# A step of fill after every step of the sample tokens' recurrence, and its eight-column products split in four

## The chip, the cores and the metric

The kernel runs on one core of one Trainium2 chip. The metric is the device time of one execution in microseconds (us), from the first to the last of the core's work. The engines carry the names of the profile: PE is TensorE's matmuls, PEld its weight loads, DVE is VectorE, ACT ScalarE, POOL GpSimd, SP SyncE. Weights and activations go through the DMA queues of SP and ACT.

## The reference, cut to what matters

One layer of a hybrid decoder works on 1024 prompt tokens and on 8 sample sequences of 4 tokens each. An FFN is followed by one wide projection `w_in`, whose columns feed four mixers (gated linear attention, a gMLP, an RWKV-7 recurrence, dilated attention); `w_out` joins them and a second FFN ends the layer. The change touches the recurrence alone, and of it the sample tokens:

```python
def step(S, xs):
    r_t, w_t, k_t, v_t, a_t, b_t = xs
    sa = jnp.einsum('bhvk,bhk->bhv', S, a_t)
    S = S * w_t[:, :, None, :] + sa[..., None] * b_t[:, :, None, :] + v_t[..., None] * k_t[:, :, None, :]
    return S, jnp.einsum('bhvk,bhk->bhv', S, r_t)
...
s_final, y = lax.scan(step, s0.astype(f32), (tm(r), tm(decay), tm(k), tm(v), tm(-kk), tm(kk * a)))
```

For the sample tokens `s0` is a given state per sequence and head (8 sequences, 4 heads, 64 x 64), and the scan has four steps.

## The kernel before, in words

**Three thirds and a fill.** The big products (`w_in`, `w_out`, the FFNs) run with the weight as the stationary operand in 128 x 128 pieces and 352 tokens as the moving one. Each product is made three times, as high part by high part, high by low and low by high (`mm3`, L131 to L145; the trace shows them as L139, L142 and L143). In `w_in` the 37 column blocks of 128 are tiles of the generator `line` (L2821): for each block and each third of the tokens, eight K pieces of three matmuls, with a yield after every second piece. So one step of this fill is 6 matmuls of 128 x 352, a third is 4 steps, and a tile is 12. After a third, `leave` (L2774) copies the result out of PSUM and stores it; during a tile the weight of the next is split by `part` (ACT L111, POOL L112) and that of the one after it is loaded. The blocks come in the order of `W_ORDER` (L2718): 8 for the recurrence, 4 for the gMLP, 6 of dilated group 2, 7 for the linear attention, then 12 of dilated groups 1 and 0, q, k and v for each pair of heads. Tile 33 waits until the recurrence and the gMLP are through (L2849, `L.mixed == 2`). Behind the last tile the fill goes on with half of `w_out`, the products `pz` at L2897 (128 x 256), and ends there; what follows has to wait for the mixers.

**The loom.** The order in which the program issues its instructions is made at build time by `Loom` (L1399). It keeps a model of when each engine is free and when each tile is written, and has a list of generators, the streams, each with a priority and a time at which it is next ready. `run` (L1574) goes round: if `cool()` says that the modelled flow of columns through TensorE in the last 3.4 us is small, it takes a step of the fill (`weft`, L1530); else the best of the streams that are ready makes a step; if none is ready, the fill makes one. On DVE and POOL the order so made is pinned in this part of the kernel (`keep(KR)`, L3088); on PE and ACT it is the order of issue, in which the build may still move single instructions.

**The recurrence.** `rwkv` (L1127) runs the prompt in four pieces of 256 tokens and the sample tokens as a fifth. Three streams are live: the two pairs of heads (`pairs(0)`, `pairs(1)`, L1340) and `feeder` (L1329), which prepares and finishes pieces. `pairs` hands each step of `unit` or `sample` on as a condition (L1354 to L1357); what these yield is used only as a further condition, and a number among it counts as none.

**The sample tokens.** `sample` (L1763) is a chain of short steps per pair: load the state (L1779), turn it (L1783), the token-by-token products (L1790), three transposes (L1795 to L1797), a 32 x 32 inverse (L1808 to L1820), its uses (L1824 to L1841), then the products of the state with the 8 columns of each sequence (L1849): for each of the two heads, 8 matmuls of 64 x 64 by 64 x 8, whose results two copies on ACT take out (L1851, L1852). The new state is made by L1856 to L1873, and L1878 to L1882 turn it and store it. There are 16 yields in it. A step's matmuls are small, its result goes through ACT or DVE before the next step can start, and the two pairs take turns, with fill between them where the loom puts it.

**What follows.** After the recurrence come the linear attention and the dilated attention (`gla`, `dil`) with the rest of the fill, at their end the sample tokens' attention over the caches (L2347, four matmuls for each of 36 loaded cache pieces), then the other half of `w_out` (L204) and the second FFN.

Of the kernel before, what the change touches and what calls it, by code (L numbers as in the profile page):

```python
# [1398 lines left out]
class Loom:  # L1399
# [4 lines left out]
    def __init__(self, tc, fill):  # L1404
        self.tc, self.ins = tc, tc.nc.cur_bb.bb.instructions
        self.i, self.last = len(self.ins), {}
        self.free, self.wrote, self.used, self.slots, self.red = {}, {}, {}, {}, {}
        self.fill, self.done, self.over = fill, {}, False
        self.live, self.hold, self.due = [], None, 0.0
        self.fresh, self.marks = [], []  # L1410
        self.ticks, self.flow, self.cells = {}, [], [0.0] * 16
        self.pe = tc.nc.tensor.engine
        self.kept = ()

    def keep(self, engines):

        self.kept = [getattr(self.tc.nc, e).engine for e in engines]
# [156 lines left out]
    def run(self, until, others=True):  # L1574

        while not until():
            now = self.free.get(self.pe, 0.0)
            if others and self.cool() and self.weft():
                continue
            ok = [s for s in self.live if others and self.open(s, now)]  # L1580
            go = [s for s in ok if s[2] <= now + SLACK]
            if go:
                self.step(min(go, key=lambda s: s[0] - (now - s[2]) / AGE))
            elif not self.weft():
                self.free[self.pe] = min(t for t in [self.due] + [s[2] for s in ok] + list(self.done.values()) if t > now)
                self.cells = [max(t, self.free[self.pe]) for t in self.cells]
# [176 lines left out]
def sample(L, rp, C, p, AR, BK, vt, eL, y, ps):  # L1763

    nc, I, O, ident = L.nc, L.I, L.O, L.ident
    D2 = dict(bufs=2)
    A, R = AR[:, 0], AR[:, 1]
    BKf = BK.rearrange("p a t -> p (a t)")
    b4 = lambda x: x.rearrange("p (b i) -> p b i", i=4)
    tri = rp.tile([32, 3, 2, 32], F32, name="tri", tag="GN0", **D2)  # L1770
    Nn, N2, IN = tri[:, 0], tri[:, 1], tri[:, 2]
    rws = rp.tile([128, 96], F32, name="rws", tag="GN1", **D2)
    RW = rws[:, 0:64].rearrange("p (b a i) -> p b a i", b=8, a=2)
    SA = rws[:, 64:96]
    S0 = rp.tile([128, 8, 64], F32, name="S0", tag="AX", **D2)
    sv = [rp.tile([64, 4, 128], F32, name="sv", tag=t) for t in ("SA2", "rE")]
    for half in range(2):
        for h in range(2):
            L.dma(sv[half][:, :, 64 * h:64 * h + 64], I["state_rwkv"][0, 4 * half:4 * half + 4, 2 * p + h].rearrange("b v k -> v b k"))  # L1779
    yield  # L1780
    q = ps("pa")
    for b in range(8):
        nc.tensor.transpose(q[:, b * 64:(b + 1) * 64], sv[b // 4][:, b % 4, :], ident[:64, :64])  # L1783
    nc.scalar.copy(S0.rearrange("p b v -> p (b v)"), q)
    work = rp.tile([128, 2, 512], F32, name="work", tag="work", **D2)
    G = work[:64, 0, 0:128].rearrange("p (h a t) -> p h a t", h=2, a=2)
    for h in range(2):
        hr = slice(64 * h, 64 * h + 64)
        q = ps("pa")
        nc.tensor.matmul(q[:64, 0:64].rearrange("p (a t) -> p a t", a=2), BKf[hr], AR[hr], start=True, stop=True)  # L1790
        nc.vector.tensor_mul(G[:, h], q[:64, 0:64].rearrange("p (a t) -> p a t", a=2), C["mS"])

    yield
    q = ps("pa")
    nc.tensor.transpose(q[:64, 0:128], BKf, ident)  # L1795
    nc.tensor.transpose(q[:32, 128:256], A, ident)
    nc.tensor.transpose(q[:64, 256:384], vt[:, 32:96], ident)  # L1797
    NB = work[:64, 0, 128:256]
    nc.scalar.copy(NB, q[:64, 0:128])
    AX = rp.tile([32, 2, 128], F32, name="AXs", tag="BK", bufs=2)  # L1800
    nc.scalar.copy(AX[:, :, 0:64], q[:32, 128:256].rearrange("p (h k) -> p h k", h=2))
    UV = rp.tile([64, 2, 64], F32, name="UVs", tag="UV", **D2)
    nc.scalar.copy(UV[32:64], q[32:64, 256:384].rearrange("p (h k) -> p h k", h=2))

    yield
    q = ps("pa")
    for h in range(2):
        nc.tensor.transpose(q[:32, h * 32:(h + 1) * 32], G[0:32, h, 0, :], ident[:32, :32])  # L1808
    nc.scalar.copy(Nn, q[:32, 0:64].rearrange("p (h t) -> p h t", h=2))
    yield  # L1810
    q = ps("pa")
    for h in range(2):
        nc.tensor.matmul(q[:32, h * 32:(h + 1) * 32], G[0:32, h, 0, :], Nn[:, h, :], start=True, stop=True)
    nc.scalar.copy(N2, q[:32, 0:64].rearrange("p (h t) -> p h t", h=2))
    nc.vector.tensor_add(IN, G[0:32, :, 0, :], ident[:32, :32].unsqueeze(1).to_broadcast([32, 2, 32]))
    yield
    q = ps("pa")
    for h in range(2):
        nc.tensor.matmul(q[:32, h * 32:(h + 1) * 32], N2[:, h, :], IN[:, h, :], start=True, stop=True)
    nc.vector.tensor_add(IN, IN, q[:32, 0:64].rearrange("p (h t) -> p h t", h=2))  # L1820
    yield
    q = ps("pa")
    for h in range(2):
        nc.tensor.matmul(q[:32, h * 64:(h + 1) * 64], G[32:64, h, 0, :], UV[32:64, h, :], start=True, stop=True)  # L1824
    nc.scalar.copy(AX[:, :, 64:128], q[:32, 0:128].rearrange("p (h k) -> p h k", h=2))
    yield
    q = ps("pa")
    for h in range(2):
        nc.tensor.matmul(q[:32, h * 128:(h + 1) * 128], IN[:, h, :], AX[:, h, :], start=True, stop=True)
    q3 = q[:32, 0:256].rearrange("p (h x) -> p h x", h=2)  # L1830
    W = work[:32, 0, 256:384].rearrange("p (h k) -> p h k", h=2)
    nc.scalar.copy(W, q3[:, :, 0:64])
    nc.scalar.copy(UV[0:32], q3[:, :, 64:128])
    yield
    q = ps("pa")
    for h in range(2):
        nc.tensor.matmul(q[64 * h:64 * h + 64, 0:32], W[:, h, :], G[0:32, h, 1, :], start=True, stop=True)
    nc.vector.tensor_add(RW[:, :, 0, :], b4(q[:, 0:32]), b4(R))
    yield
    q = ps("pa")  # L1840
    nc.tensor.transpose(q[:, 0:32], W.rearrange("p h k -> p (h k)"), ident[:32, :32])  # L1841
    nc.scalar.copy(RW[:, :, 1, :], b4(q[:, 0:32]))
    yield

    for h in range(2):
        hr = slice(64 * h, 64 * h + 64)
        q = ps("pa")
        for b in range(8):
            nc.tensor.matmul(q[hr, b * 8:(b + 1) * 8], S0[hr, b, :], RW[hr, b], start=True, stop=True)  # L1849
        q4 = q[hr, 0:64].rearrange("p (b a i) -> p b a i", b=8, a=2)  # L1850
        nc.scalar.copy(b4(y[hr]), q4[:, :, 0, :])  # L1851
        nc.scalar.copy(b4(SA[hr]), q4[:, :, 1, :])  # L1852
    yield
    q = ps("pa")
    for h in range(2):
        nc.tensor.matmul(q[64 * h:64 * h + 64, 0:32], UV[:, h, :], G[:, h, 1, :], start=True, stop=True)  # L1856
    nc.vector.tensor_add(y, y, q[:, 0:32])
    yield
    q = ps("pa")
    nc.tensor.transpose(q[:32, 0:128], SA, ident)  # L1860
    nc.vector.tensor_add(UV[0:32], UV[0:32], q[:32, 0:128].rearrange("p (h v) -> p h v", h=2))
    exs = []
    for h in range(2):
        exs.append(rp.tile([64, 8, 64], F32, name="ex", tag=("SA2", "rE")[h]))
        nc.vector.tensor_mul(exs[h], UV[:, h, :].unsqueeze(1).to_broadcast([64, 8, 64]),
                             C["bm"].unsqueeze(2).to_broadcast([64, 8, 64]))
    yield
    q = ps("pa")
    for h in range(2):
        nc.tensor.matmul(q[64 * h:64 * h + 64, :], NB[:, 64 * h:64 * h + 64], exs[h].rearrange("p b v -> p (b v)"),  # L1870
                         start=True, stop=True)
    nc.vector.tensor_add(S0, S0, q.rearrange("p (b v) -> p b v", b=8))
    nc.vector.tensor_mul(S0, S0, eL.unsqueeze(2).to_broadcast([128, 8, 64]))  # L1873
    yield
    for half in range(2):
        q = ps("pa")
        for b in range(4):
            nc.tensor.transpose(q[:64, b * 128:(b + 1) * 128], S0[:, half * 4 + b, :], ident)  # L1878
        sv = rp.tile([64, 4, 128], F32, name="svo", tag=("spread", "SA2")[half])
        nc.scalar.copy(sv, q[:64].rearrange("p (b x) -> p b x", b=4))  # L1880
        for h in range(2):
            L.put(O["s_rwkv"][0, 4 * half:4 * half + 4, 2 * p + h].rearrange("b v k -> v b k"), sv[:, :, 64 * h:64 * h + 64])  # L1882
        yield


# [1294 lines left out]
```

## Time and profile before

| | |
|---|---|
| time before, median of 3 runs | 2499.52 us (2495.64 to 2504.91) |
| the profiled execution's own time | 2503.86 us |
| its span, first to last instruction | 2502.1 us |
| PE busy over the span | 2411.0 us, 96% |
| mean granted TensorE clock | 0.972 |
| sample tokens' first state load issued | 1264.31 us |
| first and last matmul of their steps (L1783, L1878) | 1270.49 and 1317.87 us |
| end of the fill (last `pz` matmul) | about 1630.7 us |
| other half of `w_out` begins (L204) | 1680.69 us |

Times inside the execution are counted from the start of its span. A row of a windows view gives, for a stretch, its length and then for each engine the busy time and in brackets how many instructions; behind them stand the granted TensorE clock (PEclk, 1.00 is full speed), the mean busy share of the DMA engines, and GB/s. A row of a timeline gives the start, the length, the engine and line, the operation, the tiles and the shape; `x4` means four instructions of one kind merged. A matmul's length holds its way through the array, so that the distance from one start to the next is what it costs in a row of its like.

### The profile page before, as it was taken

What the parts mean: (1) busy time and instruction counts of PE and PEld (TensorE: products, weight loads), DVE (VectorE), ACT (ScalarE), POOL (GpSimd) and SP (SyncE); (2) the same over time, 40 slices, a digit from 0 to 9 for tenths busy, and PEclk for the clock granted to TensorE, in tenths of its full rate; (3) what the DMA queues carried; (4) which work ended last, traced back from release to release, by engine and by line L of the source; (5) the groups of instructions that cost most, each with busy time, mean ns of one, the idle gap of its engine ahead of it and who ended that gap; (6) DMA issues with size and microseconds to landing.
All of it is one profiled execution on the core that took longest, in us unless ns stands there. A gap on an engine that the chain in (4) does not pass through costs nothing. (4 is left out here: it accounts for less than half of the span.)

```text
span 2502.1 us, 41009 instructions
## 1 busy us (share of the span) xinstructions
PE 2411.0 (96%) x15543; PEld 2207.7 (88%) x15543; DVE 1395.5 (56%) x3211; ACT 1013.6 (41%) x2175; POOL 1067.8 (43%) x902
## 2 busy tenths in 40 slices
PE   8999999999999999999999999968999999999997
PEld 8999999977789998898888899737989999997777
DVE  7645454367775056665632467437854444447767
ACT  5433333366554242323324344415533333336651
POOL 3655555567643233232111111114355555557664
PEclk9999999999999999999989889969999999999999
DMA  4322222323434333231226676444222222233334
GB/s 133 100 69 83 66 82 68 106 86 111 119 126 132 93 106 90 87 100 52 74 56 195 185 228 184 134 130 146 79 86 74 80 74 80 72 103 92 104 103 148
DMA packets 273612, 265.21 MB, mean 106 GB/s; under 512 B 36283, under 2 KB 247380, under 8 KB 273414
## 3 DMA queue, kind: packets, MB, share of 16 engines
q1 hardware_dynamic: 223810, 212.69, 28.9%
q10 hardware_dynamic: 49604, 49.90, 5.8%
q8 instruction: 122, 2.00, 0.3%
q14 instruction: 76, 0.62, 0.1%
HBM read 195.26 MB, written 67.16 MB: 105 GB/s over the span
## 5 line engine op out<-in xcount | busy, mean ns | idle before, releaser
L520 POOL TENSOR_TENSOR wlo<-wraw,whi 128x512 fp32r<-128x512 f32 x280 | 379.7, 1374 | 355.1 <-ACT whi L519 355.0
L549 PE MATMUL p<-xh,whi 128*128 128x352 f32 x1120 | 364.0, 325 | 5.4 <-DVE hid L475 3.6
L551 PE MATMUL p<-xh,wlo 128*128 128x352 f32 x1120 | 362.3, 323 | 0.0
L550 PE MATMUL p<-xl,whi 128*128 128x352 f32 x1120 | 361.2, 322 | 0.0
L519 ACT CAST whi<-wraw 128x512 fp32r<-128x512 f32 x280 | 166.5, 620 | 409.1 <-PE p L550 293.4
L112 POOL TENSOR_TENSOR wlo<-wraw,whi 128x1024 fp32r<-128x1024 f32 x61 | 146.0, 2396 | 391.8 <-ACT whi L111 343.6
L139 PE MATMUL pw<-xh,whi 128*128 128x352 f32 x888 | 308.1, 347 | 2.3 <-ACT stg L2782 1.5
L143 PE MATMUL pw<-xh,wlo 128*128 128x352 f32 x888 | 293.4, 330 | 0.0
L142 PE MATMUL pw<-xl,whi 128*128 128x352 f32 x888 | 293.1, 330 | 0.0
L549 PEld LDWEIGHTS p<-xh,whi 128*128 128x128 f32 x1120 | 211.4, 189 | 6.8 <-DVE hid L475 3.9
L550 PEld LDWEIGHTS p<-xl,whi 128*128 128x128 f32 x1120 | 211.5, 189 | 0.0
L551 PEld LDWEIGHTS p<-xh,wlo 128*128 128x128 f32 x1120 | 210.4, 188 | 0.0
L139 PEld LDWEIGHTS pw<-xh,whi 128*128 128x128 f32 x888 | 171.5, 193 | 13.3 <-issue 7.5
L142 PEld LDWEIGHTS pw<-xl,whi 128*128 128x128 f32 x888 | 172.1, 194 | 1.9 <-issue 1.7
L143 PEld LDWEIGHTS pw<-xh,wlo 128*128 128x128 f32 x888 | 171.2, 193 | 1.4 <-issue 1.2
L549 PE MATMUL p<-hid,whi 128*128 128x352 f32 x400 | 129.9, 325 | 1.8 <-ACT n L583 1.4
L551 PE MATMUL p<-hid,wlo 128*128 128x352 f32 x400 | 129.8, 324 | 1.4 <-POOL wlo L520 1.4
L550 PE MATMUL p<-hid,whi 128*128 128x352 f32 x400 | 129.2, 323 | 0.0
L111 ACT CAST whi<-wraw 128x1024 fp32r<-128x1024 f32 x61 | 63.9, 1048 | 118.7 <-PE pw L142 85.2
L723 PE MATMUL p<-xh,hid 128*128 128x512 f32 x320 | 109.8, 397 | 0.1
L204 PE MATMUL pt<-whi,ya 128*128 128x256 f32 x512 | 97.7, 290 | 1.0 <-POOL ya L793 1.0
L839 DVE TENSOR_TENSOR y<-y,p 128x512 f32<-128x512 f32 x112 | 76.6, 685 | 38.7 <-PE p L723 36.7
(641 smaller groups left out, 5861.9 us busy)
## 6 DMA issues: line engine op xcount, KB each, us to landing
wraw<-in_w_ff_gate_dram SPq DMA_DIRECT2D x44, 512.0 KB
wraw<-in_w_ff_up_dram SPq DMA_DIRECT2D x44, 512.0 KB
wraw<-in_w_in_dram SPq DMA_DIRECT2D x37, 512.0 KB
wraw<-in_w_ff_down_dram SPq DMA_DIRECT2D x36, 512.0 KB
hid_d<-tmp ACTq DMA_DIRECT2D x60, 176.0 KB
hid_d<-n ACTq DMA_DIRECT2D x60, 176.0 KB
cv<-in_cache_win_dram SPq DMA_DIRECT2D x36, 256.0 KB
whi<-hid_d SPq DMA_DIRECT2D x32, 256.0 KB
```

Of the source, the lines that this page charges most:

```text
L112: nc.gpsimd.tensor_tensor(lo, raw, hi.bitcast(F32), op=OP.subtract)
L139: ins = nc.tensor.matmul(out, a, xh[:, cs], start=(first and i == 0), stop=False)
L142: nc.tensor.matmul(out, a, xl[:, cs], start=False, stop=False)
L143: nc.tensor.matmul(out, b, xh[:, cs], start=False, stop=(last and i == n - 1))
L204: nc.tensor.matmul(out, xs[kx][a][:, cs], ws[js[0]][b][:, kw], start=u == a == b == 0, stop=u == len(kk) - 1 and a == 1, skip_group_check= ...
L519: nc.scalar.copy(t[0][:, i], v)
L520: nc.gpsimd.tensor_tensor(t[1][:, i], v, t[0][:, i].bitcast(F32), op=OP.subtract)
L549: nc.tensor.matmul(out, ah, xh, start=first and k == 0, stop=False, skip_group_check=True)
L550: nc.tensor.matmul(out, ah, xl, start=False, stop=False, skip_group_check=True)
L551: nc.tensor.matmul(out, al, xh, start=False, stop=k == KH - 1, skip_group_check=True)
L723: nc.tensor.matmul(out, a[i][:, u], b[j][:, u], start=first and u == i == j == 0, stop=u == n - 1 and i == 1, skip_group_check=True)
L839: (nc.vector.tensor_copy if h else nc.scalar.copy)(v, p) if copy else nc.vector.tensor_add(v, v, p)
```

## The change

The loom gets a flag, `thin`. When a step of `sample` has set it, the next turn of `run` takes a step of the fill first, whatever `cool()` says. Every yield of `sample` is preceded by `L.loom.thin = True`. In the loop over the 8 sequences a yield comes after every fourth matmul, so that for each head the 8 products are issued as 4 and 4, and the 16 of a pair in four groups. The copies of a head come after its second group. This makes 20 yields of 16. Instructions, tiles and operands are the same.

```diff
@@ Loom.__init__
         self.kept = ()
+        self.thin = False
@@ Loom.run
             now = self.free.get(self.pe, 0.0)
-            if others and self.cool() and self.weft():
+            thin, self.thin = self.thin, False
+            if others and (thin or self.cool()) and self.weft():
                 continue
@@ sample: ahead of each of its 16 yields
+    L.loom.thin = True
     yield
@@ sample, the products of the state
         for b in range(8):
             nc.tensor.matmul(q[hr, b * 8:(b + 1) * 8], S0[hr, b, :], RW[hr, b], start=True, stop=True)
+            if b % 4 == 3:
+                L.loom.thin = True
+                yield 0.0
```

More of the change, by code (lines that the diff above doesn't have):

```diff
@@ L1803, in sample @@
     nc.scalar.copy(UV[32:64], q[32:64, 256:384].rearrange("p (h k) -> p h k", h=2))
+    L.loom.thin = True
     yield
@@ L1809, in sample @@
     nc.scalar.copy(Nn, q[:32, 0:64].rearrange("p (h t) -> p h t", h=2))
+    L.loom.thin = True
     yield
@@ L1815, in sample @@
     nc.vector.tensor_add(IN, G[0:32, :, 0, :], ident[:32, :32].unsqueeze(1).to_broadcast([32, 2, 32]))
+    L.loom.thin = True
     yield
@@ L1820, in sample @@
     nc.vector.tensor_add(IN, IN, q[:32, 0:64].rearrange("p (h t) -> p h t", h=2))
+    L.loom.thin = True
     yield
@@ L1825, in sample @@
     nc.scalar.copy(AX[:, :, 64:128], q[:32, 0:128].rearrange("p (h k) -> p h k", h=2))
+    L.loom.thin = True
     yield
@@ L1833, in sample @@
     nc.scalar.copy(UV[0:32], q3[:, :, 64:128])
+    L.loom.thin = True
     yield
@@ L1838, in sample @@
     nc.vector.tensor_add(RW[:, :, 0, :], b4(q[:, 0:32]), b4(R))
+    L.loom.thin = True
     yield
@@ L1842, in sample @@
     nc.scalar.copy(RW[:, :, 1, :], b4(q[:, 0:32]))
+    L.loom.thin = True
     yield
@@ L1849, in sample @@
             nc.tensor.matmul(q[hr, b * 8:(b + 1) * 8], S0[hr, b, :], RW[hr, b], start=True, stop=True)
+            if b % 4 == 3:
+                L.loom.thin = True
+                yield 0.0
         q4 = q[hr, 0:64].rearrange("p (b a i) -> p b a i", b=8, a=2)
@@ L1852, in sample @@
         nc.scalar.copy(b4(SA[hr]), q4[:, :, 1, :])
+    L.loom.thin = True
     yield
@@ L1857, in sample @@
     nc.vector.tensor_add(y, y, q[:, 0:32])
+    L.loom.thin = True
     yield
@@ L1866, in sample @@
                              C["bm"].unsqueeze(2).to_broadcast([64, 8, 64]))
+    L.loom.thin = True
     yield
@@ L1873, in sample @@
     nc.vector.tensor_mul(S0, S0, eL.unsqueeze(2).to_broadcast([128, 8, 64]))
+    L.loom.thin = True
     yield
@@ L1882, in sample @@
             L.put(O["s_rwkv"][0, 4 * half:4 * half + 4, 2 * p + h].rearrange("b v k -> v b k"), sv[:, :, 64 * h:64 * h + 64])
+        L.loom.thin = True
         yield
```

## The prediction

> **What bounds the kernel now.** I read the page first, for the span and the clock, then the windows around the sample tokens' steps, then PE's timeline there, and last the stretch in which the fill runs out.
>
> ```profile
> span 2502.1 us, 41009 instructions
> ## 1 busy us (share of the span) xinstructions
> PE 2411.0 (96%) x15543; PEld 2207.7 (88%) x15543; DVE 1395.5 (56%) x3211; ACT 1013.6 (41%) x2175; POOL 1067.8 (43%) x902
> ```
>
> PE is busy for 96% of the span, so the time is PE's work, at the clock it is granted, plus few gaps. The change moves work on PE, so two questions count: at which clock does PE run where the sample tokens are worked on, and what is it worth to have fill there instead of later? The windows answer the first.
>
> ```profile
> 1270.40:1318.40 48.00, 48.00 (x312) 38.81 (x312) 13.57 (x42) 11.42 (x37) 4.74 (x2) 0.79 0.22 62
> 1270.40:1287.90 17.50, 17.50 (x153) 14.37 (x152) 7.12 (x29) 6.00 (x22) 2.37 (x1) 0.98 0.31 87
> 1287.90:1307.60 19.70, 19.70 (x96) 14.83 (x95) 3.51 (x8) 2.96 (x11) 0.00 (x0) 0.50 0.07 20
> ```
>
> The steps of `sample` fill 48.0 us. PE never stands still in them, DVE, ACT and POOL are busy for a quarter or less, and for 19.7 us the clock is 0.50. What stands just ahead of that drop?
>
> ```profile
> 1285.22 0.51 PE L139 MATMUL pw<-xh,whi 128*128 128x352 f32 x1
> 1285.66 1.92 PE L1849 MATMUL pm<-rws,S 64*64 64x8 f32 x32
> ```
>
> Here are 32 products in a row, each of a quarter of the array and 8 columns, with one full-sized matmul of the fill ahead of them: PE is busy, the array is nearly empty. The clock falls right behind them, and the short steps that follow keep it down for 20 us. This is the place that the change goes for: with fill after every fourth product and after every other step, no such stretch is left.
>
> **The change part by part.**
>
> *The clock.* How much slower is PE at 0.50? Three pairs of rows:
>
> ```profile
> 1264.35 0.32 PE L139 MATMUL pw<-xh,whi 128*128 128x352 f32 x1
> 1264.51 0.32 PE L142 MATMUL pw<-xl,whi 128*128 128x352 f32 x1
> ```
>
> ```profile
> 1294.67 0.49 PE L139 MATMUL pw<-xh,whi 128*128 128x352 f32 x1
> 1294.96 0.49 PE L142 MATMUL pw<-xl,whi 128*128 128x352 f32 x1
> 1295.25 0.49 PE L143 MATMUL pw<-xh,wlo 128*128 128x352 f32 x1
> 1295.68 1.97 PE L1870 MATMUL pm<-ex,work 64*64 64x512 f32 x4
> ```
>
> ```profile
> 1299.88 3.18 PE L1849 MATMUL pm<-rws,S 64*64 64x8 f32 x32
> ...
> 1313.41 1.07 PE L1870 MATMUL pm<-ex,work 64*64 64x512 f32 x4
> ```
>
> A fill matmul comes every 0.16 us at full clock and every 0.29 us in the cold stretch (a ratio of 1.81), L1849 takes 3.18 instead of 1.92 us (1.66), L1870 1.97 instead of 1.07 us (1.84). Their mean is 1.77. At full clock the 19.7 us are 19.7 / 1.77 = 11.1 us: **8.6 us less**. The bounds are 19.7 - 19.7 / 1.66 = 7.8 and 19.7 - 19.7 / 1.84 = 9.0 us if the clock stays up, and 0 if it doesn't (third rival).
>
> [...]
>
> *The fill that is moved.* How much goes in? One line of the fill, L142, has two matmuls per step:
>
> ```profile
> 1264.00:1270.40 6.40, 3.54 (x11) 1.95 (x11) 1.00 0.31 78
> 1270.40:1318.40 48.00, 14.84 (x40) 9.18 (x41) 0.79 0.22 62
> 1318.40:1330.00 11.60, 6.63 (x21) 3.87 (x21) 1.00 0.24 61
> ```
>
> Weight loads of that line count 11 + 41 = 52 from the state's load to the last step, so 26 steps of fill stand beside the steps of `sample` now. After the change at least 20 per pair do, 40 in all: 14 more, of 6 matmuls at 0.16 us, **13.4 us more in this stretch**. It would be more if the loom still puts a few idle steps beside the 40, say 17 steps and 16.3 us, and less only if the build moves the fill out again.
>
> *The switches.* Going from fill to a short step and back costs this:
>
> ```profile
> 1274.82 0.32 PE L143 MATMUL pw<-xh,wlo 128*128 128x352 f32 x1
> 1275.07 0.23 PE L1808 MATMUL pm<-ident,work 32*32 32x32 f32 x2
> 1275.23 0.43 PE L139 MATMUL pw<-xh,whi 128*128 128x352 f32 x1
> 1275.50 0.32 PE L142 MATMUL pw<-xl,whi 128*128 128x352 f32 x1
> ```
>
> L1808 starts 0.25 us behind L143 where the next fill matmul would start after 0.16, and L142 starts 0.27 us behind L139 instead of 0.16: 0.09 + 0.11 = 0.20 us for each group of short matmuls. Each of the 14 steps can cut one group in two: at most **2.8 us more**; none if the step falls between groups that are apart already. I take 2.8, since the steps are put between steps by construction.
>
> *What the moved fill did where it was.* The fill has one end, so 13.4 us less of it are there at its end. What is that stretch limited by?
>
> ```profile
> 1400.00:1500.00 100.00, 99.78 (x654) 91.84 (x653) 57.10 (x180) 42.53 (x134) 13.43 (x16) 0.85 0.67 206
> 1577.00:1605.00 28.00, 27.98 (x294) 25.09 (x293) 14.35 (x48) 13.20 (x37) 4.02 (x5) 1.00 0.26 78
> 1605.00:1631.00 26.00, 26.00 (x176) 15.12 (x176) 5.35 (x22) 6.63 (x16) 2.84 (x3) 1.00 0.56 173
> ```
>
> ```profile
> 1577.00:1605.00 28.00, 9.76 (x70) 8.49 (x70) 1.00 0.26 78
> 1605.00:1631.00 26.00, 12.18 (x72) 9.25 (x72) 1.00 0.56 173
> ```
>
> ```profile
> 1593.54 0.28 PE L2897 MATMUL pz<-wlo,xl 128*128 128x256 f32 x1
> 1593.66 0.28 PE L2897 MATMUL pz<-whi,xl 128*128 128x256 f32 x1
> ```
>
> The second fence counts the fill's last products, L2897, at 0.12 us each (third fence). 13.4 us are 112 of them: all 72 behind 1605 (8.6 us) and 40 of the 70 ahead of it (4.8 us). Ahead of 1605, PE is busy for 27.98 of 28.00 us, so I let the 4.8 us come back whole. Behind 1605 the stretch belongs to the products with the loaded caches, L2347:
>
> ```profile
> 1605.00:1631.00 26.00, 11.90 (x68) 3.56 (x70) 1.00 0.56 173
> 1632.50:1645.00 12.50, 7.93 (x36) 2.04 (x36) 0.86 0.74 223
> 1645.00:1662.00 17.00, 8.43 (x36) 2.21 (x36) 0.62 0.50 154
> ```
>
> With fill beside them 68 go in 26.0 us; without fill, and the clock still mostly up, 36 go in 12.5 us, and 68 would take 23.6. So of the 8.6 us only 2.4 come back: there the fill used time that PE had free. With the clock down (36 in 17.0 us) 68 would take 32.1, and 6.1 us would be lost. I take the middle row, the nearest, since it follows right on the end of the fill: **4.8 + 2.4 = 7.2 us less**, between -6.1 and the whole 13.4.
>
> *What rides along, at nothing.* 14 steps are 3.5 thirds and a little over one tile: as many copies out, one more split of a weight, one more load on SP.
>
> ```profile
> 1310.66 0.45 ACT L2786 COPY stg<-pw 128x352 f32<-128x352 f32 x1 [3.04 <-PE pw L143]
> 1311.01 1.05 ACT L111 CAST whi<-wraw 128x1024 fp32r<-128x1024 f32 x1
> ```
>
> That is 3.5 x 0.45 + 1.05 = 2.6 us on ACT, which has 36 of its 48 us free, and a split on POOL, which has 43 free. A copy of `sample` behind the cast comes 1.05 us late; the fill step that now follows each step, 6 x 0.16 = 0.96 us, hides nearly all of it. Uncovered it is 1.05 us, once. On SP the state loads of the pairs are issued before the steps and are passed by no more than one weight load. The split adds one wait: L1851 copies a head's products only after the second four, two fill steps later, and on DVE the sum at L1857, pinned in its order, waits for it with whatever stands behind it; the other pair's steps and fill run on PE meanwhile. Without them each of the four heads would cost up to 1.9 us. The new `yield 0.0` reaches the loom through `pairs` as a plain condition, so it makes no difference that it is a number.
>
> **The sum.** -8.6 + 13.4 + 2.8 - 7.2 = +0.4 us. The profiled execution's own 2503.86 us become 2504.3. That execution lies 4.34 us above the median of the runs shown, so beside the median of 2499.52 the forecast is 2499.9, say **2500 us**. What a measurement of this kernel can tell from no change is about 0.5%, 12.5 us, so I forecast no difference.
>
> **The rivals**, each on the median:
>
> *All of the moved fill comes back.* In the stretch 1400 to 1500 PE is busy for 99.78 of 100 us; if the attention behind the sample tokens is bound by PE throughout, 13.4 us less fill make it 13.4 us shorter: -8.6 + 2.8 = -5.8, 2493.7 us. To be faster by over 12.5 us it needs 7 us more, which that stretch could give: its clock is 0.85, 15 us lost, and the loom deals its order anew. Against it speaks the waiting tail of the caches.
>
> *The tail goes cold (slower).* The fill ends before the cache products begin, the last attention steps gain nothing from that, and the clock falls under the caches as in the row with 0.62. Then the 7.2 become a loss of 6.1: -8.6 + 2.8 + 13.4 + 6.1 = +13.7, 2513.2 us. It decides if the last L2897 comes before about the first L2347. For it: 72 of 112 lie behind 1605, so the end comes near that point. Against it: the clock held 0.86 for 12 us after the fill's end.
>
> *The change does not lift the clock.* The short steps still leave the array too empty, or the build moves the fill away from them. No 8.6; of the 14 steps 19.7 / 48.0, 5.7 of them, run cold at 6 x 0.13 us more, 4.5 us: 13.4 + 2.8 + 4.5 - 7.2 = +13.5, 2513.0 us. Against it: a step brings 6 full matmuls to a few small ones, where the drop had one to 32.
>
> *The fill meets its hold.*
>
> ```profile
> c_dil_v<-stg ACTq DMA_DIRECT2D x9, 176.0 KB
> ```
>
> Nine v thirds stored by 1262 put the fill in the tile after the third v, tile 28; until the hold at 33 there are up to 60 steps. 40 and the 10.5 of 1318 to 1330 fit, with some 5 to 9 to spare. If they don't, PE has nothing beside the recurrence's last steps, up to 10.5 x 0.96 = 10.1 us, and the fill kept back serves later; at half of it, +5.5 or 2505.
>
> **How the numbers follow.** The forecast has 0.45, full return 0.26, the cold tail 0.16, no lift 0.08, the hold 0.05. Faster by over 0.5% (below 2487.0) is 0.3 of full return and 0.12 of the forecast, whose following stages are dealt anew: 0.13. Slower by over 0.5% (above 2512.0) is 0.65 of the cold tail, 0.55 of no lift and 0.05 of the rest: 0.17. The same: 0.70. The range goes from 2487, full return with 7 us of the colder stretch, to 2515, the cold tail and a little.
>
> **What would show it.** Right: PEclk near 1.00 from the first L1783 to the last L1878; this stretch 48.0 - 8.6 + 13.4 + 2.8 = 55.6 us long with some 54 loads of L142; L1849 in groups of four; the last L2897 some 15 to 30 us earlier counted from the last L1878; L204 starting at about 1681. Wrong: a clock of 0.5 in the stretch (no lift), L204 earlier by 5 us or more (full return), or PEclk under 0.7 and L2347 slower than 2.9 per us from their start (cold tail).

## The result, and the profile after

The kernel before takes 2498.61 us in the median of 12 runs (2491.58 to 2506.53), the changed one 2516.96 us of 12 (2512.99 to 2536.85). The ratio is 1.008, with an interval from 1.0062 to 1.0098: **slower by 18.4 us**, where no difference was forecast, and 2 us above the range.

The profiled execution of the changed kernel took 2535.85 us, 19 us above its median, at a mean clock of 0.967 where the median of the 12 has 0.976, so that its stage behind the sample tokens is read below only beside other runs. The page of the changed kernel:

```profile
span 2534.1 us, 41001 instructions
## 1 busy us (share of the span) xinstructions
PE 2432.6 (96%) x15543; PEld 2226.3 (88%) x15543; DVE 1402.2 (55%) x3211; ACT 1013.5 (40%) x2175; POOL 1068.9 (42%) x902
```

The work is the same (15543 matmul records in both), its share of PE too. I cut both executions in two: the *stretch*, from 6 us ahead of the first turn of a state (L1783 before, L1786 after) to 1 us behind the last store's transpose (L1878, L1897), and the *stage behind*, from there to the first L204. Windows of the kernel before, then of the changed one:

```profile
1264.50:1319.20 54.70, 54.70 (x353) 44.96 (x352) 14.66 (x45) 12.08 (x39) 4.74 (x2) 0.81 0.23 64
1319.20:1680.70 361.50, 338.12 (x2426) 282.22 (x2424) 182.12 (x636) 150.57 (x435) 52.40 (x55) 0.89 0.58 177
```

```profile
1265.30:1335.40 70.10, 70.06 (x485) 60.11 (x485) 19.31 (x49) 15.14 (x43) 10.43 (x7) 1.00 0.27 78
1289.20:1309.20 20.00, 20.00 (x142) 16.47 (x141) 5.61 (x13) 3.90 (x13) 2.38 (x1) 1.00 0.21 67
1335.40:1717.20 381.80, 344.68 (x2294) 284.54 (x2292) 184.09 (x634) 147.53 (x431) 50.92 (x51) 0.84 0.54 165
1623.40:1649.20 25.80, 23.86 (x125) 19.39 (x123) 13.19 (x43) 7.28 (x19) 3.57 (x5) 0.50 0.07 22
1649.20:1710.00 60.80, 50.50 (x241) 20.07 (x240) 20.30 (x74) 10.47 (x30) 6.71 (x9) 0.75 0.55 165
```

The clock did what was said: 1.00 through the whole stretch, also around the products (second row). But the stretch is 15.4 us longer, and the stage behind, with 132 matmul records fewer in it, is 20.3 us longer in this execution; in the median, by the table of terms below, it is about as long as before. The same windows for the fill's line L142 alone, before and then after:

```profile
1264.50:1319.20 54.70, 18.62 (x52) 11.21 (x52) 0.81 0.23 64
1319.20:1680.70 361.50, 54.27 (x155) 31.61 (x154) 0.89 0.58 177
```

```profile
1265.30:1335.40 70.10, 30.75 (x96) 18.10 (x96) 1.00 0.27 78
1335.40:1717.20 381.80, 39.05 (x111) 22.58 (x110) 0.84 0.54 165
```

With two matmuls per step, 26 steps of fill stood in the stretch before and 48 stand there now: **22 are drawn forward, not 14**. The timeline of the changed kernel at the products shows how they lie:

```profile
1290.94 0.32 PE L143 MATMUL pw<-xh,wlo 128*128 128x352 f32 x1
1291.19 0.63 PE L1861 MATMUL pm<-rws,S 64*64 64x8 f32 x8
1291.75 0.43 PE L139 MATMUL pw<-xh,whi 128*128 128x352 f32 x1
...
1292.65 0.32 PE L143 MATMUL pw<-xh,wlo 128*128 128x352 f32 x1
1292.91 0.63 PE L1861 MATMUL pm<-rws,S 64*64 64x8 f32 x8
1293.46 0.43 PE L139 MATMUL pw<-xh,whi 128*128 128x352 f32 x1
```

Each group is four products (two records each) with a step of fill on either side, where 32 records, 16 products, stood in one row.

Where PE waits most in the stage behind is told by the view of waits, of the kernel before (one row) and then of the changed one (two rows; us in total, times, longest). The merge is L2206 before and L2226 after:

```profile
PE pm L2206 <- DVE rst L1017: 4.1, 1, 4.1
```

```profile
PE pm L2226 <- DVE on L2222: 8.8, 3, 5.3
PE pm L2085 <- DVE st L2097: 5.7, 3, 3.5
```

The idle time of PE there grows from 361.5 - 338.1 = 23.4 to 381.8 - 344.7 = 37.1 us: PE now waits 8.8 us for the attention's own chain of small steps on DVE in the merge (L2226) and 5.7 in the units (L2085), where the kernel before has no such row.

### The profile page after: what moved, and what is told of

Its sections match the earlier page's. It is cut to its first block, busy times and chain, and to the rows that moved or that the text cites. A ratio compares the mean times of both kernels' runs of the same rounds, so it can differ in the third digit from the quotient of the medians.

```text
span 2534.1 us, 41001 instructions
## 1 busy us (share of the span) xinstructions
PE 2432.6 (96%) x15543; PEld 2226.3 (88%) x15543; DVE 1402.2 (55%) x3211; ACT 1013.5 (40%) x2175; POOL 1068.9 (42%) x902
## 5 line engine op out<-in xcount | busy, mean ns | idle before, releaser
L142 PE MATMUL pw<-xl,whi 128*128 128x352 f32 x888 | 290.0, 327 | 0.0
L139 PEld LDWEIGHTS pw<-xh,whi 128*128 128x128 f32 x888 | 169.5, 191 | 14.4 <-issue 6.9
L142 PEld LDWEIGHTS pw<-xl,whi 128*128 128x128 f32 x888 | 169.7, 191 | 1.3 <-issue 0.9
L204 PE MATMUL pt<-whi,ya 128*128 128x256 f32 x512 | 98.8, 292 | 1.1 <-POOL ya L793 1.1
```

Source lines behind the costliest of these rows:

```text
L139: ins = nc.tensor.matmul(out, a, xh[:, cs], start=(first and i == 0), stop=False)
L142: nc.tensor.matmul(out, a, xl[:, cs], start=False, stop=False)
L204: nc.tensor.matmul(out, xs[kx][a][:, cs], ws[js[0]][b][:, kw], start=u == a == b == 0, stop=u == len(kk) - 1 and a == 1, skip_group_check= ...
```

## The experiments

Three theories stood at first. *Lost cover*: fill drawn forward is missing behind, the time goes with how much is drawn. *Cold tail*: the clock falls when the fill ends early, and the caches' products pay for it. *Order dealt anew*: the planner, which looks at modelled times, deals another order of streams behind the recurrence, and that order costs by itself. Differences below are between the median of a kernel and that of the kernel before, measured beside it (2498.6 to 2502.1 us).

### The change again, and its parts

`after_again` is the changed kernel once more.

> The changed kernel once more, for a second trace of it (the first is of an execution 19 us above the median). Theory 1, lost cover: the fill drawn forward covered waits where it was and gives nothing back: 2513 to 2519 us, clock 1.00 through the steps of sample, 22 to 23 more steps of fill there than before, and the stage behind them not shorter than before's 362 us although it has some 21 us less fill. Theory 2, cold tail: the same time, with the clock under 0.6 where the last attention steps and the caches run, and that stage longer than before's by the cold alone, 5 us or more. Theory 3, order dealt anew: the time has nothing to do with the amount of fill; the stage behind differs in many places.

2521.0 us, +19.9, ratio 1.0078 (1.0051 to 1.0105); the same stretch of 70.1 us and 96 loads. Its stage behind is 381.9 us, again in an execution above the median (2534.37 us, clock 0.969).

`split_thin` keeps the split and the step of fill behind each group of four products, and forces no other step:

```diff
-    L.loom.thin = True
     yield
...
             if b % 4 == 3:
                 L.loom.thin = True
                 yield 0.0
```

> The eight-column products split in four with a step of fill behind each group, and no other step forced (8 forced steps instead of 40). Theory 1, lost cover: the clock stays up for most of the stretch (-6 to -9 us) and at most 8 steps, 7.7 us, are drawn forward: 2494 to 2500 us. Theory 2, cold tail: the fill still reaches the caches: 2491 to 2496 us. Theory 3, order dealt anew: anywhere from 2485 to 2520 us.

2519.39 us, +18.3, ratio 1.0072 (1.0053 to 1.009). Only 6 steps are drawn (64 loads of L142), the stretch is 53.7 us at clock 1.00, and still the cost is that of the whole change. Lost cover alone cannot do that.

`early23` leaves the recurrence as it was and forces 23 steps of fill in one go ahead of the first pair's sample steps:

```diff
                 yield from state_out(p)
+                if p == 0:
+                    L.loom.extra = 23
...
+            if self.extra and others and self.weft():
+                self.extra -= 1
+                continue
```

> The kernel before, with 23 steps of fill forced in one go just ahead of the sample steps of the first pair; no split, nothing forced in the steps themselves, so the fall of the clock stays and the amount of fill drawn forward is that of the change. Theory 1, lost cover: 23 x 0.96 = 22 us more with nothing back: 2515 to 2522 us. Theory 2, cold tail: some comes back, the tail is cold: 2508 to 2520 us, the clock under 0.6 at the end of the attention. If the stage behind were bound by PE: 2498 to 2500 us. Theory 3, order dealt anew: no tie to the amount, 2490 to 2520 us.

2538.98 us, +37.9, ratio 1.0151 (1.0131 to 1.0171), far above the 2515 to 2522 of lost cover. `early1` is the same with a single step:

> The kernel before with a single step of fill (0.95 us of PE) forced ahead of the sample tokens' steps of the first pair; all else is the planner's. Lost cover: one step, +1 us at most, 2500 to 2503 us. Order dealt anew: one step is enough to turn the planner's later choices, so the time can lie anywhere in a scatter of some 20 us, and over 5 us from the kernel before would show it; within 2 us shows nothing for or against.

2499.27 us, -1.1, ratio 0.9993 (0.9972 to 1.0014): no difference. By its timeline PE's order behind the recurrence is nearly that of the kernel before: this one step did not turn it.

### The order by itself

For these, the choices that the planner makes behind the recurrence (which stream steps, when a step of fill goes; 701 in the kernel before) were written out as a list, and a kernel can be given the list of another:

```diff
+PLAN = """
+a3 a4 a5 a7 a0 w*3 a1 a6*2 a8 a9 a2 a0 w*7 a6 a0 a6 w*3 a0 a6 w a0 w
...
         while not until():
+            if self.plan:
+                c = self.plan.pop(0)
+                if c == "w":
+                    self.due = 0.0
+                    self.weft()
+                else:
+                    s, = [s for s in self.live if s[4] == c]
+                    self.step(s)
+                continue
```

`order_thin` is the kernel before, with the list of `split_thin` behind it (the fill it lacks goes in just ahead of its last step):

> The kernel before in the recurrence, nothing split and nothing forced, but behind it the order of choices that split_thin was dealt, written out, with its 7 missing steps of fill put in just ahead of the last one. Lost cover: no step is drawn forward, so as the kernel before, 2497 to 2504 us. Order dealt anew: slower by some 10 to 18 us, 2510 to 2520 us, stage behind 370 us or more.

2514.79 us, +14.4, ratio 1.0057 (1.0039 to 1.0074): nothing is drawn forward, and most of the cost of `split_thin` is there. `order_after` does so with the changed kernel's list:

> The kernel before in the recurrence, nothing split and nothing forced, and behind it the order of choices that the changed kernel was dealt, with its 22 missing steps of fill put in just ahead of the last one. If the amount drawn forward were all: 2498 to 2503 us. If the order dealt to the changed kernel costs by itself: 2508 to 2520 us. If that order suits the smaller amount of fill only: the 22 late steps add up to 15 us in place of it, to be seen as pz ending later than 1645 us.

2513.95 us, +11.8, ratio 1.004 (1.0021 to 1.006); its last `pz` starts at 1618.0 us, so the late steps are not the reason. `head_thin` takes the list of `split_thin` up to a point at which all streams stand as in the kernel before, and then goes on as that one; `tail_thin` is the reverse. The two lists differ by 11 steps of fill at that point: `head_thin` leaves these out behind it, `tail_thin` puts them in there in one row.

> The kernel before, nothing drawn or split; behind the recurrence the first 395 choices of split_thin's order, then (the streams stand at the same steps there) the kernel before's from its 384th on, less the 11 steps of fill by which split_thin's list is ahead by then. If the cost arises at the start (first units 5 us later, and all behind them): 2509 to 2516 us as order_thin. If it arises in the second half: 2498 to 2504 us.

> The other half: the kernel before's first 384 choices, 11 steps of fill to stand level, then split_thin's order from its 395th choice on, with 7 steps of fill just ahead of the last. Cost at the start: 2498 to 2506 us (up to 5 us for the 11 steps in a row). Cost in the second half: 2509 to 2518 us.

`head_thin` 2517.72 us, +18.2, ratio 1.0072 (1.0048 to 1.0096); `tail_thin` 2510.06 us, +10.6, ratio 1.0052 (1.0033 to 1.0072). Both halves cost, and their sum is twice the whole: no one place was found for the cost, and the expectation that one half would be free fell. The 11 steps belong to what was tried, by the expectation up to 5 us of `tail_thin`. Windows of `order_thin`, `head_thin`, `tail_thin` and `order_after`, stretch and (in the first and third) stage behind:

```profile
1267.90:1317.20 49.30, 48.28 (x353) 39.88 (x352) 16.87 (x46) 12.06 (x39) 5.13 (x2) 0.97 0.25 71
1317.20:1693.60 376.40, 343.41 (x2425) 284.27 (x2423) 180.37 (x635) 151.17 (x437) 53.60 (x54) 0.89 0.57 171
```

```profile
1268.60:1317.90 49.30, 48.33 (x353) 39.95 (x352) 16.89 (x46) 12.06 (x38) 5.08 (x2) 0.97 0.25 71
```

```profile
1261.40:1309.20 47.80, 46.87 (x353) 38.68 (x352) 16.75 (x45) 12.08 (x39) 5.06 (x2) 1.00 0.26 73
1309.20:1681.90 372.70, 345.22 (x2426) 289.14 (x2424) 181.72 (x635) 151.67 (x437) 53.37 (x54) 0.90 0.56 173
```

```profile
1266.80:1321.50 54.70, 54.70 (x352) 44.96 (x352) 14.65 (x45) 12.10 (x39) 4.74 (x2) 0.81 0.23 64
```

The stage behind is 376.4 and 372.7 us long where it was 361.5, with the same work (374.2 and 374.4 in the other two). The first rows hold something else: in the stretch these four run the very program of the kernel before, and yet it is 47.8 to 54.7 us long, at a clock of 0.81 to 1.00. I come back to that.

### The amount by itself

Now the other way round: fill is drawn forward, and the list behind is the kernel before's. `replay_split` is `split_thin` with it, `replay13` the changed kernel with a cap on the forced steps, `replay` the whole change.

> The kernel with only the step of products split and followed by fill (split_thin, 7 choices of fill fewer behind the recurrence), with the order behind the recurrence written out as in the kernel before. Lost cover: as split_thin, 2514 to 2522 us, stage behind some 376 us. Order dealt anew: 2492 to 2503 us, stage behind under 364 us, since the stretch itself is 1 us shorter with 6 steps more of fill in it.

> The changed kernel with a cap on the forced steps, so that 13 steps of fill are drawn forward by the end of the sample tokens (about the 14 of the forecast), and the order behind written out as in the kernel before. By the forecast's sum (clock lifted, half of the drawn fill given back): 2499 to 2504 us. Nothing given back: 2508 to 2518 us (13 x 0.95 us, plus what a colder tail takes).

> The changed kernel, but behind the recurrence the planner no longer chooses: the 701 choices (which stream steps, and when a step of fill goes) are those of the kernel before, written out as a list. The steps of fill drawn forward stay 22, so the last 22 choices of fill in the list find nothing. Lost cover (time goes with the amount of fill drawn forward): as the change, 2514 to 2523 us, and the stage behind 375 us or more. Order dealt anew: most of the cost goes with the order, 2496 to 2508 us, stage behind under 368 us. Sample stretch 70 us at clock 1.00 by both.

| | drawn, by L142 | stretch | stage behind | time | ratio |
|---|---|---|---|---|---|
| `replay_split` | 6 | 53.7 | 361.2 | 2506.22, +5.8 | 1.0017 (0.9997 to 1.0037) |
| `replay13` | 12 | 61.2 | 361.7 | 2513.51, +11.4 | 1.0047 (1.0031 to 1.0064) |
| `replay` | 22 | 70.1 | 375.8 | 2533.64, +33.3 | 1.0129 (1.0102 to 1.0157) |

With the order held, 12 steps cost nearly their own time, 0.96 us each, and 22 cost more. The 5.8 us of the 6 steps are not clear of noise, and the split alone costs as much (`split_replay`, below). In none of the three profiles is the stage behind shorter by the fill that is gone. For `split_thin`, the order of the kernel before takes 12 of its 18 us away; for the change it makes things worse by 13 to 15 us. So a dealt order can be good or bad for the fill it meets, and "the new order is worse" is too simple.

`dummies` has the long stretch without drawing the fill: 20 of the forced steps issue six products that nobody reads.

```diff
+            if thin and others:
+                self.thins += 1
+                if self.thins % 2 and self.fakes < 24:
+                    self.fakes += 1
+                    self.fake()
+                    continue
...
+            for u in range(6):
+                nc.tensor.matmul(p, xs2[0][0][:, 0:128], xs2[u][0][:, third(0)], start=u == 0, stop=u == 5)
```

> The changed kernel in which 20 of the forced steps do not draw fill but six unread 128x352 products of the same length (0.95 us of PE), so that only 2 steps of fill stand forward; the order behind written out as in the kernel before. The stretch beside the sample tokens is as long as in the change (70 us at clock 1.00). If the drawn steps are simply not given back: as replay, 2528 to 2538 us. If the stage behind misses them (its clock): it is now as in the kernel before, 357 to 362 us, and the time 2514 to 2522 us, some 14 us under replay, though the fill is all still to do.

2521.95 us, +22.5, ratio 1.01 (1.0078 to 1.0121). Windows of `replay`, then of `dummies`:

```profile
1263.30:1333.40 70.10, 70.06 (x485) 60.11 (x484) 19.28 (x49) 15.15 (x43) 10.43 (x7) 1.00 0.27 78
1333.40:1709.20 375.80, 342.04 (x2293) 284.38 (x2292) 177.42 (x633) 148.01 (x431) 46.46 (x50) 0.85 0.54 165
```

```profile
1266.40:1334.70 68.30, 68.30 (x475) 58.53 (x475) 16.11 (x43) 12.60 (x40) 4.75 (x2) 1.00 0.18 50
1334.70:1699.50 364.80, 335.47 (x2407) 283.96 (x2406) 181.45 (x636) 150.72 (x434) 53.14 (x55) 0.92 0.56 175
```

With about the same stretch, the stage behind takes 364.8 us with nearly all of its fill still to do (54 loads of L142 in the stretch, one step more than before), and 375.8 with 22 steps less. And the change itself (+18.4 and +19.9) is not faster than this to any extent that the intervals could tell: the drawn fill is worth little more than useless work in its place.

One thing goes with all these times: an execution's mean clock. Of the 12 executions of the changed kernel the fastest, 2512.99 us, has 0.979 and the slowest, 2536.85 us, 0.968. A line through the 77 executions of the kernel before whose clock is on record (2489.58 to 2513.12 us) falls by 1.7 us for each 0.001. `replay` has 0.970 in its median and `dummies` 0.9765; by that line, an estimate, 11 of the 11.7 us between the two go with the clock. That the clock is the cause of it is not shown.

### Is it PE's work or the clock at the end?

`less_z` is the kernel before without 99 of the fill's last 432 products, 11.9 us of PE; the layer's outputs lack that part of the sum.

```diff
-                    for a, b in ((0, 0), (0, 1), (1, 0)):
+                    for a, b in ((0, 0), (0, 1), (1, 0)) if q < 3 else ((0, 0),) if u == 0 else ():
...
-                    if u % 2:
+                    if u % 2 and q < 3:
```

> The kernel before with the last quarter of the fill's w_out products left out but for one matmul of each token block (99 of 432 matmuls, 11.9 us at 0.12 us each; the output leaves that part of the sum out). Nothing is drawn forward; the fill is only shorter at its end. Theory 1, lost cover: nothing gained, 2496 to 2500 us. Theory 2, cold tail: slower, 2501 to 2510 us, the clock down before the caches end. If PE bound that stage: 2487 us. Theory 3: 2485 to 2515 us.

2504.55 us, +3.5, ratio 1.0013 (1.0 to 1.0026). 11.9 us less to do, and nothing gained. Two things go with it: its mean clock is 0.970 in the median, where the kernel before has 0.975 beside it, some 8 us by the line above; and the planner deals the order anew from the missing steps on, for no list holds it here. So what the lighter work gave may have been lost in these. Windows of the stretch, of the time from the fill's end to the caches' first product, and of these products:

```profile
1264.00:1314.90 50.90, 49.95 (x354) 40.94 (x353) 17.04 (x47) 12.10 (x39) 5.08 (x2) 0.93 0.25 69
...
1594.80:1614.00 19.20, 18.65 (x105) 13.53 (x107) 5.43 (x18) 7.38 (x22) 1.76 (x4) 0.51 0.15 44
1614.00:1667.00 53.00, 42.94 (x228) 17.86 (x227) 13.88 (x55) 10.05 (x25) 6.18 (x7) 0.82 0.60 192
```

Behind the fill's end the clock is 0.51 over 19.2 us, as it was 0.50 over 25.8 us in the changed kernel. Does the loss lie in that fall? `replay_more` fills the 22 empty choices of `replay` with unread products, `tail_fill` deals them without end behind the fill of the kernel before:

```diff
         yield "end"
+        while L.mixed < 3:
+            p = L.ps.tile([128, 256], F32, name="pz", tag="pw", bufs=2)
+            for u, k in enumerate(K3[:2]):
+                for a, b in ((0, 0), (0, 1), (1, 0)):
+                    nc.tensor.matmul(p, xs3[k][a][:, 0:128], W[nn + 3][b][:, u], start=u == a == b == 0, stop=u == 1 and a == 1)
+            yield
```

> The kernel of replay (22 steps of fill drawn forward, order behind as in the kernel before), with 22 steps of six 128x256 products that nobody reads put in where its list finds no fill any more: some 16 to 21 us more work for PE, and nothing else. If the drawn fill is missed because it kept the clock up (cover by clock): the added work costs nothing or less, 2518 to 2534 us, and PEclk of the stage behind rises from 0.85 to 0.90 or more. If PE's amount of work sets the end: 2549 to 2555 us.

> The kernel before, with steps of the same unread products dealt by the planner without end behind the last step of fill, until the attention's streams are through. Cold tail (the clock, 0.64 in the kernel before at 1642 to 1694 us, sets the time of the caches' products): 5 to 10 us faster, 2490 to 2496 us. Tail set by the transfers and the chain of small steps: within 3 us of the kernel before, or slower by up to 10 us, where the unread products stand in front of others on PE.

`replay_more` 2544.29 us, +42.2, ratio 1.0172 (1.0156 to 1.0189), 8.9 us more than `replay`; `tail_fill` 2510.53 us, +8.4, ratio 1.0033 (1.0015 to 1.0051). Stretch and stage behind of `tail_fill`, and stage behind of `replay_more`:

```profile
1262.80:1313.60 50.80, 49.85 (x353) 40.84 (x352) 16.90 (x46) 12.15 (x39) 5.07 (x2) 0.93 0.25 69
1313.60:1698.20 384.60, 367.85 (x2659) 311.48 (x2658) 184.52 (x647) 152.58 (x440) 53.58 (x55) 0.93 0.56 174
```

```profile
1333.40:1722.10 388.70, 358.06 (x2425) 300.00 (x2424) 177.22 (x633) 148.16 (x431) 46.68 (x50) 0.87 0.52 159
```

With more work the clock of the stage is a little higher (0.93 for 0.89, 0.87 for 0.85, one execution each), and it does not pay. PE's work alone is not it either, for then 22 steps would have cost 16 to 21 us and not 8.9. Both expectations for `replay_more` were missed. The cold tail as the cause finds no support in these two, but they don't rule out a share of it: the unread products take PE's time themselves.

`split_replay`, last, has the split, no forced step, and the list of the kernel before:

> The kernel before with the step of products split in four and no step forced (the planner itself puts 3 steps of fill fewer beside the sample tokens), the order behind written out as in the kernel before, with those 3 steps just ahead of the last. If the clock is lifted by the split alone: the stretch 46 to 50 us at 0.95 or more, and 2494 to 2500 us, up to 8 us under the kernel before. If the clock falls all the same, or is lifted in most executions of the kernel before already (49 to 51 us in four of six profiled ones): 2498 to 2504 us, no gain.

2505.32 us, +5.8, ratio 1.0028 (1.0012 to 1.0044). Stretch and stage behind:

```profile
1263.10:1313.60 50.50, 49.53 (x334) 41.93 (x334) 16.01 (x45) 11.58 (x38) 4.77 (x2) 0.83 0.24 66
1313.60:1690.60 377.00, 346.97 (x2443) 290.91 (x2442) 184.57 (x636) 151.00 (x436) 52.50 (x55) 0.89 0.55 170
```

The split without the fill gains nothing, and its clock is 0.83. The profiled execution (2514.52 us) lies 9 us above its median, and its stage behind is 377.0 us under the list with which `replay_split` took 361.2: single stages of one execution are no finer than that, and the stages above bear weight only where the medians say the same. None of these kernels beats the kernel before; `early1` and `replay_split` are not told apart from it.

## Why the prediction was wrong, step by step

| term | forecast | measured | from |
|---|---|---|---|
| clock lifted | -8.6 | -3.3 | 47.8 us at clock 1.00 (`tail_thin`) against 51.1, the mean of seven executions |
| fill drawn forward | +13.4 | +21.1 | 22 steps of 0.96 us |
| switches | +2.8 | +1.2 | 70.1 - 47.8 - 21.1 |
| given back behind | -7.2 | -0.6 | the rest to +18.4 |
| sum | +0.4 | +18.4 | |

Three terms failed, all to the same side: the drawn fill by 7.7 us, what it gives back by 6.6, the clock by 5.3. The last row but one is what is left of the median when the others are taken off; a changed order is in it.

**The clock.** Its sign came true: with a step of fill behind the groups, or of unread products in its place, it is 1.00 in the stretch of all eight profiled kernels that have it, with the split alone 0.83. That fill would hold it up was the author's estimate from the 0.50 behind the products; why the clock falls there no run shows, and without any forced step behind the products `tail_thin` has 1.00 too. (The "32 products in a row" were 16, each in two records.) The size was taken from one profiled execution, and that was one of the bad ones. The same program stands in the stretch of seven profiled kernels: 54.7 us (before, `order_after`), 50.9 (`less_z`), 50.8 (`tail_fill`), 49.3 (`order_thin`, `head_thin`) and 47.8 (`tail_thin`), the rows above, 51.1 in the mean. Even from the slowest of them, lifting gains 54.7 - 47.8 = 6.9 and not 8.6 us. One and the same order, in the middle of a kernel, had 0.81, 0.93, 0.97 and 1.00; what makes the difference the traces do not show.

**The fill that is moved.** This is the step that failed first: "After the change at least 20 per pair do, 40 in all: 14 more". The planner's own steps go on beside the forced ones, 8 in all, and 48 stand there. The forecast had let them be "say 17 steps" of drawn fill, still 5 too few. The "some 54 loads" among its signs was a slip: 41 and 2 x 14 are 69 by its own count. The part of the stretch that it spoke of holds 85 loads and is 63.4 us long (1271.2 to 1334.6), not 55.6.

**The switches** are 0.06 us a step rather than 0.20.

**What the moved fill did where it was.** "Ahead of 1605, PE is busy for 27.98 of 28.00 us, so I let the 4.8 us come back whole": a busy PE was taken for one that is bound by its work. `replay13` drew about the forecast's own amount under the old order and cost +11.4, with a stage behind of 361.7 us for 361.5; `less_z` took 11.9 us from there and gained nothing, though with another order at its end and a lower clock. PE's busy time holds matmuls that are stretched by a half clock (0.50 with PE busy for 23.86 of 25.80 us; in the kernel before a fill matmul came every 0.16 us at a clock of 1.00 and every 0.29 us at 0.50). That the chain of the attention's small steps ends the stage while fill covers it is argued from the waits at L2085 and L2226, not shown. The measured value, 0.6 us given back, lies midway between the 7.2 and the bound of -6.1.

**What rides along at nothing** held in the stretch: ACT has 15.1 and POOL 10.4 busy us of 70.1, and PE stands still for 0.04. But the sentence that the following stages "are dealt anew" stood only in the chance of a faster result. `order_thin` and `order_after` price it at +14.4 and +11.8 us.

**The rivals.** Full return is out, and so is a clock not lifted, and the hold (PE is busy throughout). The cold tail had the right sign, 2513.2 us, and its point came: the last L2917 ends at about 1623.6 and the first L2367 starts at 1649.2. These products go slowly at first, by the windows of the changed kernel for L2367 alone:

```profile
1649.20:1674.00 24.80, 12.01 (x50) 3.27 (x50) 0.63 0.40 122
1674.00:1710.00 36.00, 19.98 (x94) 5.28 (x94) 0.84 0.65 195
```

That is 2.0 a us at 0.63 and then 2.6 at 0.84, under its 2.9. Yet its mechanism does not carry the cost of the change: over all executions the mean clock is the same (0.975 in the median of those 77 of the kernel before, 0.976 of the 12 changed ones).

**The signs** that came true: PEclk near 1.00, the groups of four, and the fill's end 23.6 us earlier counted from the last transpose (289.2 for 312.8). L204 started at 1717.2 and not at 1681, in an execution 19 us above the median.

**What stays open.** Why `replay`, with 22 steps less fill behind the stretch and under the same order, takes 11.7 us longer than `dummies` (its lower clock goes with it, but what lowers it and whether that is the cause wasn't tried); why the stage gives nothing back in the change itself, where amount and order act together; and which of the dealt choices cost 10 to 18 us. Each half of one list costs 10 us or more, so a single choice in one half does not explain it. Whether another order for the changed kernel would be faster wasn't tried.

## What to carry to other kernels

Work that is pulled forward to fill a gap has to be counted as the scheduler will really deal it, forced steps and its own together, and costs its full time unless a run shows that the place it came from gets shorter; a PE that is busy there proves nothing, since leaving out 11.9 us of its work gained no time here. Where a greedy planner orders the rest by modelled times, an edit ahead of it can deal a new order, and that alone was worth up to 18 us here: hold the order by a written list before an edit's own effect is read. And a half clock in one profiled execution has to be seen in a second one before its whole length is booked as a gain; the mean clock of every execution, beside its time, tells whether the profiled one is like the rest.

## What the runs showed of the hardware

The granted clock in one unchanged program order went from 0.81 to 1.00 between executions, 6.9 us in a stretch of 50. It does not follow PE's busy share: 0.50 with PE busy for 19.70 of 19.70 us in the short steps of the kernel before, 1.00 with 70.06 of 70.10 us in the stretch that has a step of fill between all short ones. And the time of an execution goes with its mean clock: 2512.99 us at 0.979 and 2536.85 at 0.968 for one kernel.
